# Own tokens' queries ahead of the dense ones, 432 dense columns, and GpSimd on nine pairs' low parts

## The chip, the cores and the metric

One Trainium2 chip, of which the kernel uses one core. The metric is the device time of one launch in microseconds. Engines are named as in the profile: PE is TensorE (PEld its weight loads), DVE is VectorE, ACT is ScalarE, POOL is GpSimd, SP is the engine that issues most transfers.

## The reference

One layer of a streaming encoder over 640 tokens: 512 of a prompt and 128 of eight short samples. A recurrent group and an attention group are merged into h; then each token picks experts. Only that second half changes here:

```python
xn = rmsnorm(h, ln2_g)                                     # 640 x 1024
q = (xn @ w_query).reshape(T, 8, 2, 128)                   # w_query 1024 x 2048
s1 = einsum('thd,kd->thk', q[:, :, 0], sub_keys1)          # 128 keys for each half
s2 = einsum('thd,kd->thk', q[:, :, 1], sub_keys2)
# top 16 of each half, top 16 of the 256 sums: 16 of 16384 experts for each of 8 heads
gates = softmax(top_s)
act = gelu(einsum('thkd,td->thk', u[idx], xn))
y = h + einsum('thk,thkd->td', gates * act, v[idx])
```

## The kernel before

The tokens are five tiles of 128: prompt tiles 0 to 3, and tile 4 with the samples. They take one of two ways through the experts.

*Dense tokens.* The first SD = 448 tokens of the prompt multiply all 16384 experts. The experts come in 64 pairs of 128-column blocks. In the **U stage** (loop over c in 0..63) a pair's weights, 128x2048, are loaded (`u_load`), rounded by ScalarE into the high part wh (`high`, L95) and subtracted into the low part wl (`low`, L100); both together are a `put`. `u_block` (L960) multiplies each block in 24 matmuls of 448 columns: wh with the high and the low part of the tokens, wl with the high part. ScalarE applies gelu into `act`, which goes to memory (Ad). In the **V stage** the same is done for V: activations and gate weights come back (at, gt), are multiplied (`weigh`) and split (`weigh_split`: ph, pl), and `expert_out` (L1359) accumulates 48 matmuls of 448 columns a pair into eight banks. Tiles wh, wl and raw have two buffers each.

*Gate weights.* `select(t)` finds a tile's sixteen experts for each head; `matrix(t)` spreads the weights into a 128x128 map for each token in blocks of eight (`hot` on VectorE, `place` on TensorE, `store` on ScalarE). These pieces have costs in us, and a plan distributes them over the steps of the U loop.

*Own tokens.* The last 64 prompt tokens (HD) and the 128 samples gather their experts' rows instead: for each of NR = 128 + 64 slots GpSimd gathers a row for each partition (`fetch`, L1174), VectorE multiplies it with the token's row (L1181, dots), and later adds the weighted V rows (L1186). A prompt token takes two partitions with 64 rows each, a sample one with 128. `own_work` issues about three gathers a step into a ring of six buffers and consumes those of the step before.

*The query stage* stands ahead of U. Eight slabs of w_query (128x2048, two halves u of 128 columns each) multiply all 640 tokens: `proj_T` (L113) issues 48 matmuls of 320 columns for each u. Behind them `query_keys(u - 2)` scores the queries of two blocks ago against the keys (L914, five tiles), ScalarE copies the scores (L916), VectorE searches them (five instructions a tile). Then, for even u, `next_slab(G)` rounds the next slab on ScalarE and makes its low part on GpSimd; at last `query_out` copies the queries out of PSUM. Each engine runs its instructions in the order in which the code issues them. GpSimd makes the low parts of the query slabs and of the pairs up to 3, VectorE the others.

Of the kernel before, what the change touches and what calls it, by code (L numbers as in the profile page):

```python
# [7 lines left out]
F32 = mybir.dt.float32  # L8
# [8 lines left out]
P = 128  # L17
# [18 lines left out]
SD = S - HD  # L36
# [12 lines left out]
def hybrid_layer(ctx: ExitStack, tc: tile.TileContext, i, o):  # L49
# [144 lines left out]
    for k in range(KD):  # L194
# [19 lines left out]
        + [i["w_out"][n] for n in range(4)] + [i["w_query"][n] for n in range(PH)]  # L214
# [603 lines left out]
    X3 = dram.tile([HD, D], F32, name="X3")  # L818
# [21 lines left out]
    for t in range(NT):  # L840
        merge_attn(0, t)
    next_slab(V)
    for t in range(ND):
        merge_attn(1, t)
        nc.sync.dma_start(Hd[t], h_rows[:, t])
        if t:
            scaled(t - 1)
        mean_square(t)
    merge_attn(1, 4)
    xh, xl = parts_tile()  # L850
    two = [wide(), wide()]
# [25 lines left out]
    sp_ = ctx.enter_context(tc.tile_pool(name="own", bufs=1))  # L877

# [5 lines left out]
    for r in (0, HD):  # L884
        nc.sync.dma_start(xrow[r:r + HD, 1], X3)
    NR = PH * TK + HD
# [3 lines left out]
    ring2 = sp_.tile([P, RING - ND + 1, D], F32, name="ring2")  # L890
    ap_ = ctx.enter_context(tc.tile_pool(name="ap", bufs=2))
# [8 lines left out]
    tq, close_tq = open_pool("tq")  # L900
    qt = {}

    def query_out(u, ps):
        q = qt[u] = tq.tile([P, T], F32, name="q", tag="q", bufs=2)
        A.activation(q.rearrange("p (a b) -> p a b", a=2), ps[:, :, :H2], AF.Copy)

    def query_keys(u):
        c, n = u // 2, u % 2
        s = tq.tile([P, NT, NK], F32, name="s", tag="s", bufs=2)
        q = qt.pop(u)  # L910
        for t0, t1 in ((0, 4), (4, 5)):
            sc = bank()[:, :(t1 - t0) * P]
            for t in range(t0, t1):
                PE.matmul(sc[:, (t - t0) * P:(t - t0 + 1) * P], q[:, t * P:(t + 1) * P], sk[n],  # L914
                          start=True, stop=True)
# [549 lines left out]
```

## Time and profile before

| | |
|---|---|
| timed runs | 1716.91, 1719.96, 1726.47 us (median 1719.96) |
| profiled execution | 1711.95 us, of it span 1710.2 us |
| TensorE busy | 1679.2 us, 98% |
| VectorE, GpSimd, ScalarE busy | 1417.1, 690.2, 679.6 us |
| moved by DMA | 492.67 MB, mean 288 GB/s |
| mean granted TensorE clock | 0.994 of 2.4 GHz |

A line of the profile names an instruction by its line in the kernel, its engine, its operation and its tiles, output first. A matmul's length includes the time through the array, so that neighbours overlap: how fast they follow each other is read from their starts. Lengths on VectorE overlap a little as well. "waits" and "<-" name what an instruction waited for.

### The profile page before, as it was taken

The page shows a single profiled execution, that of the slowest core. Times are in us where ns is not written, and L with a number is a line of the kernel's source. Part 1 is how long each engine was busy: PE and PEld are TensorE (multiplying, and loading weights), DVE is VectorE, ACT ScalarE, POOL GpSimd, SP SyncE. Part 2 cuts the span into 40 slices and gives each one's busy share as a digit, 9 for nine tenths or more (in the row PEclk, how much of TensorE's full clock was granted, in tenths as well). Part 3 has the DMA queues.
Part 4 walks back from the last instruction along what each step waited for, and adds up shares of the span by engine and source line. Part 5 has one row for each costly group of instructions (what it writes and reads, how often), then busy time and mean ns, then how long its engine had stood idle before and what let it go on. Part 6 is the DMA issues. An engine that isn't in the chain of part 4 may idle for free.

```text
span 1710.2 us, 24851 instructions
## 1 busy us (share of the span) xinstructions
PE 1679.2 (98%) x9654; PEld 1546.7 (90%) x9654; DVE 1417.1 (83%) x2348; ACT 679.6 (40%) x790; POOL 690.2 (40%) x485
## 2 busy tenths in 40 slices
PE   8999999999999999999999999899999999999998
PEld 8887889999989898999899999899998999999998
DVE  7766465999789999899988885788887888888886
ACT  5457332233444544554455553322232232232322
POOL 4122003233134344444444433455454555455551
PEclk9999899999999999999999999999999999999999
DMA  5313233223689898999999999999999999999995
GB/s 169 104 48 113 76 105 90 75 70 126 249 277 322 308 377 291 370 389 348 314 379 344 372 352 403 397 380 368 384 374 335 405 376 385 375 377 376 369 350 201
DMA packets 180983, 492.67 MB, mean 288 GB/s; under 512 B 16817, under 2 KB 75057, under 8 KB 170225
## 3 DMA queue, kind: packets, MB, share of 16 engines
q1 hardware_dynamic: 124848, 288.68, 46.7%
q0 software_dynamic: 55296, 201.35, 31.4%
q8 instruction: 75, 1.23, 0.3%
q10 hardware_dynamic: 720, 1.05, 0.2%
q14 instruction: 44, 0.35, 0.1%
HBM read 426.11 MB, written 65.48 MB: 287 GB/s over the span
## 4 chain that ended last, share of the span: by engine, by line
PE 75%; DVE 14%; DMA 5%; ACT 3%; issue 2%; POOL 0%; DVEq 0%; ACTq 0%; SPq 0%
PE po L1359 35%; PE pa L960 21%; PE pa L113 7%; PE pb L1134 3%; DVE wl L100 2%; DMA gt<-Gd 2%; PE pb L638 2%; PE pa L638 2%; DVE ring L1181 2%; DVE h_rows L1181 2%; DMA raw<-in_u 2%; PE pb L914 1%; PE pa L857 1%; ACT wh L95 1%; DMA Gd<-stage 1%
## 5 line engine op out<-in xcount | busy, mean ns | idle before, releaser
L1359 PE MATMUL po<-ph,wh 128*128 128x448 f32 x1024 | 374.7, 366 | 3.5 <-ACT act L1280 1.9
L1359 PE MATMUL po<-pl,wh 128*128 128x448 f32 x1024 | 374.9, 366 | 3.2 <-DVE pl L1273 3.2
L100 DVE TENSOR_TENSOR wl<-raw,wh 128x2048 fp32r<-128x2048 f32 x135 | 308.8, 2288 | 83.5 <-ACT wh L95 82.8
L960 PE MATMUL pa<-xh,wh 128*128 128x448 f32 x1024 | 377.5, 369 | 0.0
L1359 PE MATMUL po<-ph,wl 128*128 128x448 f32 x1024 | 374.5, 366 | 0.0
L960 PE MATMUL pa<-xh,wl 128*128 128x448 f32 x1024 | 374.2, 365 | 0.2 <-DVE wl L100 0.2
L960 PE MATMUL pa<-xl,wh 128*128 128x448 f32 x1024 | 374.1, 365 | 0.0
L95 ACT ACTIVATE wh<-raw 128x2048 fp32r<-128x2048 f32 x146 | 279.5, 1914 | 226.9 <-PE po L1359 173.8
L1174 POOL DMA_INDIRECT h_rows<-in_u_rows,rowi x96 | 138.5, 1443 | 219.9 <-DVE h_rows L1181 164.1
L1174 POOL DMA_INDIRECT ring<-in_u_rows,rowi x96 | 136.8, 1425 | 194.3 <-DVE ring L1181 173.4
L1174 POOL DMA_INDIRECT h_rows<-in_v,rowi x96 | 155.9, 1624 | 143.4 <-DVE h_rows L1186 121.3
L1359 PEld LDWEIGHTS po<-ph,wh 128*128 128x128 f32 x1024 | 192.7, 188 | 19.5 <-ACT act L1280 2.2
L1359 PEld LDWEIGHTS po<-pl,wh 128*128 128x128 f32 x1024 | 192.7, 188 | 19.0 <-DVE pl L1273 3.8
L960 PEld LDWEIGHTS pa<-xh,wl 128*128 128x128 f32 x1024 | 192.3, 188 | 16.1 <-DVE wl L100 0.6
L1359 PEld LDWEIGHTS po<-ph,wl 128*128 128x128 f32 x1024 | 192.7, 188 | 15.3
L960 PEld LDWEIGHTS pa<-xh,wh 128*128 128x128 f32 x1024 | 192.4, 188 | 15.2 <-ACT act L1280 0.3
L960 PEld LDWEIGHTS pa<-xl,wh 128*128 128x128 f32 x1024 | 192.5, 188 | 15.1
L1174 POOL DMA_INDIRECT ring<-in_v,rowi x96 | 149.8, 1560 | 133.2 <-DVE h_rows L1186 109.2
L1280 ACT ACTIVATE act<-pa 128x448 f32<-128x448 f32 x128 | 71.5, 559 | 232.4 <-PE pa L960 225.1
L1271 ACT ACTIVATE ph<-at 128x896 fp32r<-128x896 f32 x64 | 61.0, 953 | 254.0 <-DVE at L1266 254.0
L1142 ACT ACTIVATE stage<-pb 128x512 f32<-128x512 f32 x112 | 109.8, 1129 | 89.9 <-PE pb L1134 89.9
L1273 DVE TENSOR_TENSOR pl<-at,ph 128x896 fp32r<-128x896 f32 x64 | 69.9, 1093 | 72.7 <-ACT ph L1271 72.7
(280 smaller groups left out, 2498.7 us busy)
## 6 DMA issues: line engine op xcount, KB each, us to landing
raw<-in_u SPq DMA_DIRECT2D x64, 1024.0 KB
raw<-in_v SPq DMA_DIRECT2D x64, 1024.0 KB
Ad<-act SPq DMA_DIRECT2D x64, 448.0 KB
Gd<-stage SPq DMA_DIRECT2D x28, 1024.0 KB
gt<-Gd SPq DMA_DIRECT2D x64, 448.0 KB
at<-Ad SPq DMA_DIRECT2D x64, 448.0 KB
raw<-in_w_query SPq DMA_DIRECT2D x8, 1024.0 KB
raw<-in_w_out SPq DMA_DIRECT2D x4, 1024.0 KB
```

Of the source, the lines that this page charges most:

```text
L95: A.activation(wh, raw, AF.Copy)
L100: eng.tensor_sub(wl, raw, wh.bitcast(F32))
L113: PE.matmul(ps[:, hf, :H2], a[:, k, cs], b[:, k, hf * H2:(hf + 1) * H2], start=(k == 0 and n == 0), stop=(k == KD - 1 and n == 2))
L638: PE.matmul(ps, a[:, k0 + k, ts_], b[:, k, :], start=(k == 0 and n == 0), stop=(k == CT - 1 and n == 2))
L960: PE.matmul(u_ps[c, n][:, :SD], a[:, k, n * P:(n + 1) * P], b[:, k, :SD], start=(k == 0 and m == 0), stop=(k == KD - 1 and m == 2))
L1142: A.activation(d["stage"][:, :, t0:t0 + 4].rearrange("p j t -> p t j"), d[n, f], AF.Copy, scale=1.0 / GSC)
L1174: G.indirect_dma_start(out=rows[n], out_offset=None, in_=table, in_offset=bass.IndirectOffsetOnAxis(ap=rowi[:, c:c + 1], axis=0))
L1181: V.scalar_tensor_tensor(row, row, 1.0, xrow[:, n // NS_], op0=ALU.mult, op1=ALU.mult, accum_out=dots[:, n:n + 1])
L1271: A.activation(ph, a2, AF.Copy)
L1273: V.tensor_sub(pl, a2, ph.bitcast(F32))
L1280: A.activation(act[c][:, n], u_ps[c, n][:, :SD], AF.Gelu_apprx_tanh)
L1359: PE.matmul(po[k][:, :SD], a[:, j, k * P:(k + 1) * P], b[:, j, :], start=(c == 0 and j == 0 and n == 0), stop=(c == NS - 1 and j == 1 and ...
```

## The change

Own tokens are now the 128 samples, the last 64 prompt tokens as before, and sixteen more prompt tokens ahead of these (NC). These sixteen gather by head: partition h*16 + t holds head h of token t, in sixteen more slots. Dense tokens are the first 432.

The queries are made in two passes over the eight slabs, which are loaded and split twice: first the 256 columns of tiles 3 and 4 (OWN), then the 384 of tiles 0 to 2 (DENSE). The rows of tiles 3 and 4 are normalised and transposed first. The samples' selection runs in the second pass, and the first ten gathers are issued there. Scores of the dense tiles are held in the buffers of `stage`, and searched partly in the second pass, partly as seven more pieces of the plan. GpSimd makes the low parts of the expert pairs up to 9. The multiplies of the sixteen tokens need the rows by head (`rows_by_head`, eight transfers in the U loop); their sums over heads are made by way of memory (Yc) in the V loop.

```diff
-SD = S - HD
+NC = 16
+C0 = P - HD - NC
+SD = S - HD - NC
...
-        + [i["w_out"][n] for n in range(4)] + [i["w_query"][n] for n in range(PH)]
+        + [i["w_out"][n] for n in range(4)] + [i["w_query"][n] for _ in range(2) for n in range(PH)]
...
+    turns = (ND - 1, ND) + tuple(range(ND - 1))
...
+    OWN, DENSE = slice((ND - 1) * P, T), slice(0, (ND - 1) * P)
+    def queries(ps, w, n, cols):
+        wh, wl = w
         for k in range(KD):
             for m, (a, b) in enumerate(((wh, xh), (wh, xl), (wl, xh))):
+                PE.matmul(ps[:, :cols.stop - cols.start], a[:, k, n * P:(n + 1) * P], b[:, k, cols],
                           start=(k == 0 and m == 0), stop=(k == KD - 1 and m == 2))
...
+    turn_rows(ND - 1)
+    turn_rows(ND)
+    scaled(turns[-1])
     for n in range(2):
+        queries(two[n], kc(slabs[A0 + 2]), n, OWN)
+        turn_rows(n)
+    turn_rows(2)
...
-    for u in range(2, 2 * PH):
-        c, n = u // 2, u % 2
-        ps = wide()
-        proj_T(ps, kc(slabs[Q0 + c]), xh, xl, n)
-        query_keys(u - 2)
-        if n == 0:
-            if c + 1 < PH:
-                next_slab(G)
...
-        query_out(u, ps)
...
+    for u in range(2, 2 * PH):
+        ps = wide()[:, 0]
+        queries(ps, kc(slabs[Q0 + u // 2]), u % 2, OWN)
+        own_keys(u - 2)
+        if u % 2 == 0:
+            next_slab(G)
+        query_out(u, ps, OWN)
+    todo, acts, sought, used = list(own_first), [], 0, 0.0
+    for u in range(2 * PH):
+        c, n = u // 2, u % 2
...
+        queries(ps, kc(slabs[Q0 + PH + c]), n, DENSE)
+        if u < 2:
+            own_keys(2 * PH - 2 + u)
+        else:
+            scores(u - 2 + 2 * PH, 3, later(u - 2))
+        for f in acts:
+            f()
+        if n == 0:
+            if c + 1 < PH:
+                next_slab(G)
...
+        query_out(u + 2 * PH, ps, DENSE)
+        used = max(used, 0.0) - 4.2
+        while used < 0:
+            if todo:
+                p = todo.pop(0)
+                p[2]()
...
+            elif sought < u - 2:
+                search(sought, tiles, held_s[sought])
...
+        if not todo:
+            own_step(n_pre, n_pre + 1)
+            n_pre += 1
...
+            if n == NB_ - 1:
+                rows_by_head()
...
+            if c == NR - 1:
+                nc.sync.dma_start(Yc.rearrange("h (t q) d -> (h t) (q d)", t=NC), y)
+                parts = p2.tile([P, PH, P], F32, name="parts", tag="y2")
+                nc.sync.dma_start(parts, Yc.rearrange("h r d -> r h d"))
+                rest = p2.tile([P, 2, P], F32, name="rest")
...
+                V.tensor_reduce(rest[:, 1], parts.rearrange("p h d -> p d h"), axis=AX.X, op=ALU.add)
+                V.tensor_add(rest[:, 0], rest[:, 0], rest[:, 1])
...
-            put(*((U, c + 1) if c + 1 < NS else (Pv, 0)), G if c <= 2 else V)
+            put(*((U, c + 1) if c + 1 < NS else (Pv, 0)), G if c <= 8 else V)
```

ScalarE's order in the query stage, before, from the rounding of one slab to that of the next (s are scores, q queries, wh a slab's high part):

```order
L95 ACTIVATE wh<-raw 128x2048
L905 ACTIVATE q<-pa 128x640
L916 ACTIVATE s<-pb 128x512
L916 ACTIVATE s<-pb 128x128
L905 ACTIVATE q<-pa 128x640
L916 ACTIVATE s<-pb 128x512
L916 ACTIVATE s<-pb 128x128
L95 ACTIVATE wh<-raw 128x2048
```

The same of the changed kernel in the pass over the own columns (the tile act now holds queries, out of pa, and scores, out of pb):

```order
L97 ACTIVATE wh<-raw 128x2048
L932 ACTIVATE act<-pa 128x256
L940 ACTIVATE act<-pb 128x256
L932 ACTIVATE act<-pa 128x256
L940 ACTIVATE act<-pb 128x256
L97 ACTIVATE wh<-raw 128x2048
```

The sequence is the same, with 256 columns where there were 640; the rounding stands behind a copy of scores in both.

GpSimd's order before, from its last low parts to the gathers of the first steps:

```order
L100 TENSOR_TENSOR wl<-raw,wh 128x2048 x2
L1174 DMA h_rows<-in_u_rows,rowi 128x1024 x3
L1174 DMA ring_2608<-in_u_rows,rowi 128x1024 x3
L1174 DMA h_rows<-in_u_rows,rowi 128x1024 x3
L1174 DMA ring_2608<-in_u_rows,rowi 128x1024 x3
```

And of the changed kernel, from the end of the second query pass into the U loop:

```order
L102 TENSOR_TENSOR wl<-raw,wh 128x2048
L1185 DMA h_rows<-in_u_rows,rowi 128x1024
L1185 DMA ring_2561<-in_u_rows,rowi 128x1024
L102 TENSOR_TENSOR wl<-raw,wh 128x2048
L1185 DMA ring_2561<-in_u_rows,rowi 128x1024 x2
L1185 DMA h_rows<-in_u_rows,rowi 128x1024
L102 TENSOR_TENSOR wl<-raw,wh 128x2048
L1185 DMA h_rows<-in_u_rows,rowi 128x1024 x2
```

Low parts and gathers now alternate, where all low parts stood ahead of all gathers.

VectorE's order in the V loop of the changed kernel, at the sixteen tokens' last sum (yc is their sum, parts what comes back from memory):

```order
L102 TENSOR_TENSOR wl<-raw,wh 128x2048
L1351 TENSOR_TENSOR at<-at,gt 128x864
L1358 TENSOR_TENSOR pl<-at,ph 128x864
L1202 SCALAR_TENSOR_TENSOR yc<-ring_2561,slots,yc 128x1024
L1215 TENSOR_REDUCE rest<-parts 128x128
L1216 TENSOR_TENSOR rest<-rest 128x128
L1202 SCALAR_TENSOR_TENSOR h_rows<-h_rows,slots 128x1024 x2
L102 TENSOR_TENSOR wl<-raw,wh 128x2048
L1351 TENSOR_TENSOR at<-at,gt 128x864
```

The reduction and the addition behind it are new; the low part of the next pair and its weighing stand behind them.

## Rows read from the trace of the kernel before

**Rows 1.** Stage by stage; times in us, TensorE clock, DMA share.
```profile
core 0: us, PE busy (x) PEld busy (x) DVE busy (x) ACT busy (x) POOL busy (x), PEclk, DMA share, GB/s
268.00:383.00 115.00, 115.00 (x822) 115.00 (x821) 96.86 (x522) 31.96 (x50) 32.39 (x7) 1.00 0.20 66
383.00:1071.00 688.00, 681.50 (x3993) 626.73 (x3991) 608.79 (x1129) 328.03 (x344) 278.02 (x192) 1.00 0.91 327
1071.00:1703.00 632.00, 626.85 (x3091) 580.01 (x3091) 535.00 (x416) 185.24 (x136) 319.22 (x201) 1.00 0.96 366
620.00:1000.00 380.00, 377.97 (x2353) 348.53 (x2352) 349.19 (x503) 194.99 (x204) 164.59 (x113) 1.00 0.98 351
```

**Rows 2.** First and last dense matmul of each stage, durations in ns.
```profile
L960 PE MATMUL pa<-xh,wh x1024: 362/365/472, 383.0 to 1068.6; 128*128 128x448 f32 x171
...
L1359 PE MATMUL po<-ph,wh x1024: 362/365/575, 1071.3 to 1702.2; 128*128 128x448 f32 x171
```

**Rows 3.** Timeline of one slab's period in the query stage; start, length in us.
```profile
267.94 0.46 PE L113 MATMUL pa<-xh,wh 128*128 128x320 f32 x2
...
274.98 1.27 PE L914 MATMUL pb<-sk,q 128*128 128x128 f32 x10
276.07 0.77 ACT L916 ACTIVATE s<-pb 128x512 f32<-128x512 f32 x2 [7.23 <-PE pb L914]
276.72 1.92 ACT L95 ACTIVATE wh<-raw 128x2048 fp32r<-128x2048 f32 x1
278.71 4.63 POOL L100 TENSOR_TENSOR wl<-raw,wh 128x2048 fp32r<-128x2048 f32 x1 [11.53 <-ACT wh L95]
...
284.17 0.54 PE L113 MATMUL pa<-xh,wh 128*128 128x320 f32 x2
```

**Rows 4.** GpSimd's low parts, shortest, median and longest in ns.
```profile
L100 POOL TENSOR_TENSOR wl<-raw,wh x11: 4612/4626/4649, 262.5 to 406.3; 128x2048 fp32r<-128x2048 f32 x11
```

**Rows 5.** Timeline, starts of matmuls of 256, 512, 320 and 448 columns.
```profile
100.08 0.28 PE L186 MATMUL pb<-wl,xh 128*128 128x256 f32 x1
...
102.60 0.28 PE L186 MATMUL pb<-wl,xh 128*128 128x256 f32 x1
...
227.81 1.07 PE L638 MATMUL pb<-wh,xl 128*128 128x512 f32 x4
...
230.53 1.07 PE L638 MATMUL pa<-wh,xl 128*128 128x512 f32 x4
...
274.69 0.46 PE L113 MATMUL pa<-xh,wl 128*128 128x320 f32 x2
...
1199.82 0.36 PE L1359 MATMUL po<-pl,wh 128*128 128x448 f32 x1
...
1204.48 0.36 PE L1359 MATMUL po<-ph,wh 128*128 128x448 f32 x1
```

**Rows 6.** Chain of waits, TensorE's placing of two blocks in the U stage.
```profile
689.44 1.85 PE pb L1134 x32
```

**Rows 7.** Timeline, ScalarE spreading a selection.
```profile
430.78 3.70 ACT L1048 ACTIVATE ix<-it 128x2048 f16<-128x2048 f16 x2
```

**Rows 8.** Stretches around a fall of TensorE's clock, columns as Rows 1.
```profile
160.00:165.00 5.00, 2.96 (x23) 1.66 (x21) 4.13 (x8) 3.24 (x5) 5.00 (x8) 1.00 0.98 359
165.00:170.00 5.00, 4.37 (x9) 2.01 (x8) 5.00 (x5) 4.97 (x14) 2.15 (x2) 0.60 0.58 211
170.00:175.00 5.00, 5.00 (x74) 4.25 (x74) 4.72 (x9) 0.12 (x1) 0.00 (x0) 0.50 0.01 3
```

**Rows 9.** Groups by line, VectorE, 620 to 1000 us.
```profile
L100 DVE TENSOR_TENSOR wl<-raw,wh 128x2048 fp32r<-128x2048 f32 x35 | 80.1, 2290 | 26.6 <-ACT wh L95 26.1 <-issue 0.4
...
L1181 DVE SCALAR_TENSOR_TENSOR h_rows<-h_rows,xrow 128x1024 f32<-128x1024 f32 x56 | 66.4, 1222 | 0.0
```

**Rows 10.** Timeline, VectorE in V behind a transfer.
```profile
1312.39 1.22 DVE L1190 TENSOR_TENSOR h_rows<-h_rows,y 64x1024 f32<-64x1024 f32 x1 [3.00 <-DMA y<-h_rows]
```

**Rows 11.** Instructions on one tile, 400 to 412 us, lengths in ns.
```profile
L1004 DVE TENSOR_TENSOR cand<-val x4: 209/312/4659, 406.4 to 411.5; 128x128 f32<-128x128 f32 x2, 128x192 f32<-128x192 f32 x1, 128x64 f32<-128x64 f32 x1
```

More of the change, by code (lines that the diff above doesn't have):

```diff
@@ L1149, in matrix, with later, rest_of_plan @@
             piece(2.4, lambda n=n: hot(n), pe=lambda n=n: place(n), act=lambda n=n: store(n))
-    for t in (ND, ND - 1):
-        select(t)
-    n_own = len(pieces)
-    select(0)
-    matrix(ND - 1)
-    select(1)
-    matrix(0)
-    select(2)
-    matrix(1)
-    matrix(2)
+    select(ND)
+    own_first = pieces[:]
+    del pieces[:]
+    held, held_s = [], {}
+    def later(u):
+        if u == 2 * PH - 1:
+            held_s[u] = qs[u + 2 * PH][:, 3 * P:6 * P]
+        else:
+            if u % 5 == 0:
+                held.append(tb.tile([P, NK, TG], F32, name="stage", tag="stage", bufs=3)
+                            .rearrange("p a b -> p (a b)"))
+            held_s[u] = held[u // 5][:, u % 5 * 3 * P:(u % 5 + 1) * 3 * P]
+        return held_s[u]
+    def rest_of_plan():
+        select(ND - 1)
+        select(0)
+        matrix(ND - 1)
+        select(1)
+        matrix(0)
+        select(2)
+        matrix(1)
+        matrix(2)
     NO = 2 * NR
-    NS_ = PH * TK
     rows = {}
@@ L1198, in hybrid_layer, with own_step @@
     NS = NK // 2
[L1201 to L1229 removed]
+    n_pre = 0
+    def own_step(n0, n1):
         for n in sorted(rows):
@@ L1235, in own_work, with own_keys @@
             fetch(n)
+    def own_work(c):
+        own_step(*[n_pre + min(NO - n_pre, (NO - n_pre) * x // (2 * NS - 2)) for x in (c, c + 1)])
+    Q0 = A0 + 2
+    own_tiles, tiles = (ND - 1, ND), tuple(range(ND - 1))
+    def own_keys(u):
+        s = qs[u][:, 2 * P:4 * P]
+        scores(u, 2, s)
+        search(u, own_tiles, s)
+    next_slab(G)
+    for u in range(2):
+        query_out(u, two[u], OWN)
+    for u in range(2, 2 * PH):
[5 more added lines that the diff above has]
+        query_out(u, ps, OWN)
@@ new lines, in hybrid_layer @@
+    put(U, 1, G)
+    scores(4 * PH - 2, 3, later(2 * PH - 2))
+    u_block(0, 0)
+    scores(4 * PH - 1, 3, later(2 * PH - 1))
+    for u in (2 * PH - 1, *range(sought, 2 * PH - 1)):
+        piece(5.0, lambda u=u: search(u, tiles, held_s[u]))
+    rest_of_plan()
+    plan = [[] for _ in range(NS + 4)]
+    total = sum(p[0] for p in pieces)
+    used, c = 0.0, 0
+    for p in pieces:
+        while used >= total * (c + 1) / (NS - 6):
+            c += 1
+        plan[c].append(p)
+        used += p[0]
+        if p[5]:
+            c += 1
```

175 lines of the change are left out of this document (79 added, 96 removed).

## The prediction

> **What bounds the kernel now.** I read the table of stages first, then the first and last dense matmuls, then the query stage instruction by instruction, then what VectorE and GpSimd do beside the dense stages.
>
> [rows 1] is to be read as three stages. In the query stage (268 to 383 us) TensorE is busy for all of 115.0 us; in the U stage (383 to 1071) for 681.5 of 688; in the V stage (1071 to 1703) for 626.85 of 632. [rows 2] gives the same borders from the matmuls themselves. So TensorE bounds all three, and each matmul made shorter is a gain as long as nothing else becomes late. What could become late is to be seen in [rows 1] and [rows 3]. In the U stage VectorE has 349.19 us of work in a stretch of 380, the DMA engines a share of 0.91 to 0.98. In the query stage the slab chain is nearly as long as TensorE's own work: TensorE starts a slab at 267.94, its scores at 274.98; ScalarE copies the scores at 276.07, only then rounds the next slab (276.72, 1.92 us), GpSimd starts on the low part at 278.71 and ends at 283.34, and TensorE takes up that slab at 284.17. That chain has 0.83 us to spare in a slab period of 16.23 us. TensorE does not wait there today only because a slab gives it sixteen microseconds of matmuls.
>
> **The change, part by part.**
>
> *Columns.* 3072 matmuls of U and 3072 of V go from 448 to 432 columns. The starts in [rows 5] give the pitch: 256 columns 120.0 ns (21 steps from 100.08 to 102.60), 512 columns 226.7 ns (12 steps), 320 columns 146.7 ns (46 steps from 267.94 of [rows 3] to 274.69), 448 columns 202.6 ns (23 steps). The first three are exactly 32 columns more than the width at 2.4 GHz; 448 is 2.6 ns above that. I keep the 2.6 ns and take 16/2.4 = 6.67 ns off each: 6144 x 6.67 ns = -41.0 us. Ends: -37 by the slope from 448 to 512 (6.0 ns), -57 if 432 lands on the rule (193.3 ns, so 9.3 ns).
>
> *Placing.* Two of the 56 blocks of eight tokens go. Two blocks cost 1.85 us of TensorE [rows 6]: -1.9 us.
>
> *Query stage.* This is the large term. The queries are now done in two passes over the same eight slabs, 256 own columns first, then 384 dense ones, and each slab is loaded, rounded and split twice. The order on ScalarE has not changed in kind: copy of the scores, rounding of the next slab, copy of the queries. So the next slab's rounding still waits until TensorE has done one query block and the scores behind it, but TensorE has now only the second block with which to cover rounding and low part. The period from one slab's low part to the next's, own pass: 22 remaining matmuls x 0.120 = 2.64, scores of two tiles 0.51 (ten instructions take 1.27 [rows 3]), hand-over 0.07, copy of 256 columns 0.30 (640 take 0.65), rounding and hand-over 1.99, low part 4.63 ([rows 4]: 4,612 to 4,649 ns in all eleven), 0.05: 10.2 us, against 6.8 us of TensorE's work. Dense pass: 22 x 0.1733 = 3.81, scores 0.76, 0.07, 0.40, 1.99, 4.63, 0.05: 11.7 us against 9.8. ScalarE also spreads the selection of the sample tile ahead of one rounding, 3.7 us [rows 7]. The first slab that the loop makes is ready at about 268 in both kernels, for its rounding stands behind the copies of the last transposes in both. So U starts at 268 + 7 x 10.2 + 8 x 11.7 + 3.7 = 437, not 383.0: +54 us. Nothing hides this: TensorE's next instruction needs that slab. Ends: +11 if no slab were late (7 x 6.8 + 8 x 9.8 = 126 us instead of 115), +54 otherwise. I take +54, since each link of the chain has its row.
>
> *TensorE's clock.* The own pass leaves gaps of 3.4 us in every 10.2. The nearest rows are [rows 8]: after five microseconds in which TensorE was busy for 2.96 the granted clock went from 1.00 to 0.60 in the next five and 0.50 (1.2 GHz) in those after. At 1.2 GHz an own period would be 22 x 0.12 + 0.51 = 3.15 us longer. Ends 0 and 7 x 3.15 = +22; I take +3, one period, for the gap ahead of the first slab that the loop makes, which is twice as long.
>
> *U stage.* Nine pairs' low parts (2.29 us each on VectorE, three of them on GpSimd already) leave VectorE, 16 more gathers and seven leftover searches come in. Behind the ninth pair VectorE's work per pair is what it was: 349.19 us over 35 pairs ([rows 1], [rows 9]), 9.98 us, plus 0.2 because by the planner's own costs 256.6 units fill 58 steps where 203.4 filled 48. TensorE's pair falls from 380/35 = 10.86 to 10.54. The margin goes from 0.88 to 0.36 us a pair. Today TensorE idles 6.5 us in this stage; with the margin more than halved I take that to grow by as much again and a little, +8 us. Ends: -6.5 (the relief of nine pairs removes all waits) and +20.
>
> *Transfers that VectorE now waits for.* Between dots 192 and 193 eight transfers rewrite the own rows; the next multiply waits for them. In V the 16 gathered tokens' sums go to memory and back, two transfers one behind the other, before a VectorE reduction; queued behind that reduction are the next pair's low part and weighing, and TensorE waits for those. The nearest row is the one transfer of that kind that there is: VectorE sat 3.00 us [rows 10]. I take +3 for the first (0 to 10) and +8 for the second, two such waits of double size less the slack of a pair (3 to 20).
>
> *Nothing.* The earlier start of the gathers, the 8 MB of second slab loads and the GpSimd gathers between low parts are hidden: the loads have a 10 us period at 66 GB/s [rows 1], and in the dense pass GpSimd has 4.63 + 2 gathers in 11.7 us.
>
> *Sum.* -41.0 - 1.9 + 54 + 3 + 8 + 3 + 8 = +33.1 us. On the profiled execution's 1711.95 us (span 1710.2) that is 1745 us. The timed runs of before lie at 1716.9 to 1726.5, their median 8.0 above the profiled execution, so I expect 1753 us in timed runs.
>
> **Rivals.**
>
> *The slabs are not late* (faster). TensorE's work is all that counts, as today, where the stage has no idle microsecond [rows 1]. Then +54 and +3 become +11: -41 - 1.9 + 11 + 19 = -13, 1699, timed 1707. It decides if the slab period is under 6.8 and 9.8 us; for that the rounding would have to run before the scores' copy, and the order says otherwise. Against it stands the 0.83 us that the chain has to spare now.
>
> *It comes back in the dense stages* (no change). The columns cost 193.3 ns (-57) and the relief of VectorE takes away the waits of U (-6.5) and most of the transfers' (+5): -57 - 1.9 + 57 - 6.5 + 5 = -3, timed 1717. The 2.6 ns above the rule speak for it, VectorE's share for the rest of U against it.
>
> *GpSimd holds VectorE* (slower still). The one VectorE instruction with two inputs from SBUF that met a low part on GpSimd lasted 4,659 ns where its fellows last about 0.3 us [rows 11]; it ended with the low part. If the row multiplies of the pairs 1 to 8 are held like this, each pair has 3.8 us of multiplies (3.2 of 1.19 us, [rows 9]), 4.1 of search (three tiles; in the query stage 70 tiles took 96.86 us [rows 1]) and up to 4.63 of holding, 12.5 us against TensorE's 48 x 0.196 = 9.4: 8 x 3.1 = +25, timed 1778. It decides where VectorE has no search to put beside the low part; the order puts the multiplies right behind it, so I expect most of the holding to fall where a search would have run anyway.
> The Trainium skill's GPSIMD Engine Reference, section Specifications, says that GpSimd's way into SBUF is shared with VectorE and that instructions with two SBUF inputs contend for it. By that rule every row multiply beside a low part would wait, and the time would be the 1778 us of this rival; the trace agrees with its 4,659 ns for one instruction, and shows no row multiply in that place.
>
> *The DMA engines become the bound* (slower still). V moves 366 GB/s at a share of 0.96 [rows 1]. If that is the most they give, 16 more gathers of 0.52 MB less 2 MB of narrower tiles are 6 MB, 16 us, and V takes 648 us instead of 632 - 20: +36, timed 1789. That TensorE idles only 5 us in V today, at whatever rate the transfers ask for, speaks against it.
>
> **Chances.** Forecast 0.64, slabs not late 0.08, comes back 0.12, GpSimd holds 0.10, DMA 0.06. The forecast alone runs from 1725 (columns at -57, the small terms at their low ends less half) to 1780 (clock and U at their high ends). The range for all is 1718 to 1788. About 0.5%, 8.6 us, is what a measurement of this kernel can tell from no change. Faster 0.08; same 0.11, from the third case and the forecast's edge; slower 0.81.
>
> **What would show it.** TensorE's busy time between the first own query and the first 432-column matmul should be about 70 to 85% with gaps ended by GpSimd's low part, 3.4 us each in the own pass and 1.9 in the dense; the first 432-column matmul should start near 437; 432 columns should have a pitch of 195.9 ns; U should take about 674 us and V about 620; GpSimd's 25 low parts should last 4.6 us each. I am wrong if TensorE stays busy through both passes, if the pitch is not between 193 and 197, or if the pairs 1 to 8 of U take 12 us and more.

## The result and the profile after

The changed kernel took 1787.11 us (median of four runs, 1777.9 to 1791.96) against 1721.49 us before (median of four, 1716.91 to 1726.47): a ratio of 1.037 with a 95% interval of 1.032 to 1.043. Slower was forecast and slower it is, but 1753 us was too little: the measured change, 65.6 us, is twice the forecast one. Its profiled execution took 1789.18 us, 77.2 us above that of before.

The table of stages of the changed kernel, for the stretches that answer to [rows 1], columns as there:

```profile
268.00:454.70 186.70, 144.84 (x873) 140.89 (x873) 118.49 (x549) 53.19 (x78) 78.11 (x24) 0.88 0.30 108
454.70:1151.00 696.30, 668.04 (x3956) 632.27 (x3955) 622.36 (x1157) 316.91 (x335) 340.12 (x218) 0.99 0.95 339
1151.00:1780.00 629.00, 610.99 (x3085) 584.12 (x3086) 532.90 (x404) 182.80 (x134) 309.15 (x201) 0.98 0.96 365
```

and the first and last dense matmul of each stage, answering to [rows 2]:

```profile
L958 PE MATMUL pa<-xh,wh x1024: 351/360/710, 454.7 to 1149.8; 128*128 128x432 f32 x171
...
L1444 PE MATMUL po<-ph,wh x1024: 351/358/729, 1151.2 to 1780.1; 128*128 128x432 f32 x171
```

The query stage was without an idle microsecond before. Now TensorE is busy for 144.8 of its 186.7 us, at a mean granted clock of 0.88. Counting 48 matmuls to a pair in the timeline splits the whole difference:

| from, to | before | after | change |
|---|---|---|---|
| start to first U matmul | 383.0 | 454.7 | +71.7 |
| U, 64 pairs | 686.4 | 695.9 | +9.5 |
| between U and V | 1.9 | 0.6 | -1.3 |
| V, 64 pairs | 631.7 | 629.6 | -2.1 |
| behind V | 7.3 | 6.6 | -0.7 |

An undisturbed pair takes 9.40 us in U and 9.36 in V, where it took 9.73 in both: 64 x (0.33 + 0.37) = 44.8 us that the columns do bring. U and V together are 7.4 us longer all the same, so 52 us are lost in them again. Most of it, some 40 us, lies in pairs that stand far apart: of U those that start at 587, 601, 614 and 1085 us (14.1, 13.1, 13.6 and 18.5 us), of V those at 1334, 1349, 1390 and 1407 (14.2, 13.2, 17.3 and 12.9).

**The slab chain**, answering to [rows 3]. One undisturbed period of the pass over the own columns, timeline, start and length in us:

```profile
306.07 0.39 PE L866 MATMUL pa<-xh,wl 128*128 128x256 f32 x1 [3.32 <-POOL wl L102]
308.81 0.61 PE L939 MATMUL pb<-sk,act 128*128 128x128 f32 x4
309.45 0.39 ACT L940 ACTIVATE act<-pb 128x256 f32<-128x256 f32 x1 [6.24 <-PE pb L939]
309.74 1.91 ACT L97 ACTIVATE wh<-raw 128x2048 fp32r<-128x2048 f32 x1
311.72 4.53 POOL L102 TENSOR_TENSOR wl<-raw,wh 128x2048 fp32r<-128x2048 f32 x1 [5.70 <-ACT wh L97]
316.30 0.39 PE L866 MATMUL pa<-xh,wl 128*128 128x256 f32 x1 [3.33 <-POOL wl L102]
```

The links follow one another as in [rows 3], but the period is now the chain's own length, 10.23 us, and TensorE waits 3.33 us in it. What was not expected is what happens to periods like this one elsewhere. Three stretches of ten microseconds of the changed kernel, columns as above:

```profile
280.00:290.00 10.00, 8.24 (x48) 8.24 (x49) 3.58 (x20) 2.35 (x3) 1.80 (x2) 0.66 0.29 105
310.00:320.00 10.00, 6.67 (x57) 6.47 (x56) 5.95 (x32) 2.88 (x6) 4.53 (x1) 1.00 0.31 97
430.00:440.00 10.00, 10.00 (x52) 10.00 (x52) 3.86 (x17) 2.67 (x3) 3.25 (x3) 0.83 0.56 210
```

At 280 us and again at 430 the mean clock lies between its two levels (0.5 would be 1.2 GHz all through). The matmuls ahead of the scores then take longer, and the scores, the copy, the rounding and the low part all come later: the slab chain starts on TensorE, so a slow TensorE lengthens it. Three of the seven own periods took 11.6 to 12.7 us and six of the dense ones 13.3 to 14.0, where the chain alone makes 10.2 and 11.8 (the latter from e2 below).

**The exchange by way of memory in V**, timeline of the changed kernel:

```profile
1390.29 0.32 SPq L1210 DMA_DIRECT2D Yc<-yc  x1
1392.93 0.37 SPq L1212 DMA_DIRECT2D parts<-Yc  x1
1398.00 1.96 DVE L1215 TENSOR_REDUCE rest<-parts 128x128 f32<-128x1024 f32 x1 [7.74 <-DMA parts<-Yc]
1400.00 0.29 DVE L1216 TENSOR_TENSOR rest<-rest 128x128 f32<-128x128 f32 x1
1400.32 0.34 SPq L1217 DMA_DIRECT2D out_y<-rest  x1
1400.75 0.39 SPq L92 DMA_DIRECT2D raw<-in_v  x1
1401.19 0.66 SPq L1340 DMA_DIRECT2D gt<-Gd  x1
1404.93 1.05 DVE L1351 TENSOR_TENSOR at<-at,gt 128x864 f32<-128x864 f32 x1
1406.15 0.92 ACT L1356 ACTIVATE ph<-at 128x864 fp32r<-128x864 f32 x1 [14.36 <-DVE at L1351]
1407.12 0.73 PE L1444 MATMUL po<-ph,wh 128*128 128x432 f32 x1 [7.74 <-ACT ph L1356]
```

VectorE waits 7.74 us for the transfer, and TensorE waits as long, 7.74 us, nine microseconds later, for what stood behind the reduction on VectorE: low part and weighing. SyncE is held too, from 1393.9 to 1400.3, by the store of the sum, and the next loads stand behind it; no run separates this hold from VectorE's wait. The pair after the wait takes 12.9 us instead of 9.4, at a clock of 0.74. The other exchange, that of the prompt's last tokens ([rows 10], 3.00 us there), does the same at 1348.58: TensorE waits 4.12 us, and the next pair takes 13.2.

**Small transfers in U.** The sixteen tokens' slots and rows are spread over the heads by transfers of their own:

```profile
594.65 5.24 SPq L1088 DMA_DIRECT2D slots<-ts  x8
...
600.57 5.22 SPq L1088 DMA_DIRECT2D rowi<-ti  x8
605.88 0.53 SPq L92 DMA_DIRECT2D raw<-in_u  x1
...
611.89 1.91 ACT L97 ACTIVATE wh<-raw 128x2048 fp32r<-128x2048 f32 x1 [9.98 <-DMA raw<-in_u]
...
614.27 0.47 PE L958 MATMUL pa<-xh,wh 128*128 128x432 f32 x1 [3.53 <-ACT act L1365]
```

SyncE issues one in 0.65 us; with two more of their kind they keep it for twelve microseconds, and a slab of U is asked for only behind them. ScalarE has nothing to round for 9.98 us. And at the rows by head:

```profile
1081.44 4.39 SPq L893 DMA_DIRECT2D xrow<-X  x8
...
1092.34 1.23 DVE L1192 SCALAR_TENSOR_TENSOR h_rows<-h_rows,xrow 128x1024 f32<-128x1024 f32 x1 [10.93 <-DMA Gd<-stage]
...
1096.03 1.25 PE L1131 MATMUL pb<-ow,oh 128*128 128x128 f16 x10 [6.27 <-DVE ow L1123]
```

The multiply reads xrow and a gathered row, never Gd: the transfer named in the bracket is only the one that ended nearest. It waits for the eight copies ahead of it, 10.93 us, and the placing that TensorE waits for stands behind it on VectorE.

**GpSimd**, one of the pairs 3 to 10 of U:

```profile
485.20 1.97 POOL L1185 DMA_INDIRECT ring<-in_u_rows,rowi  x1 [0.30 <-issue]
487.47 0.93 POOL L1185 DMA_INDIRECT h_rows<-in_u_rows,rowi  x1 [0.30 <-DVE s L925]
488.41 4.63 POOL L102 TENSOR_TENSOR wl<-raw,wh 128x2048 fp32r<-128x2048 f32 x1
491.00 3.14 DVE L1192 SCALAR_TENSOR_TENSOR ring<-ring,xrow 128x1024 f32<-128x1024 f32 x1
493.20 1.77 POOL L1185 DMA_INDIRECT h_rows<-in_u_rows,rowi  x1 [0.16 <-issue]
495.27 1.97 POOL L1185 DMA_INDIRECT h_rows<-in_u_rows,rowi  x1 [0.30 <-issue]
497.54 0.93 POOL L1185 DMA_INDIRECT ring<-in_u_rows,rowi  x1 [0.30 <-DVE s L925]
498.49 4.62 POOL L102 TENSOR_TENSOR wl<-raw,wh 128x2048 fp32r<-128x2048 f32 x1
```

From one low part to the next GpSimd has 10.08 us without a pause: 4.63 and three gathers, two of which take 1.8 to 2.0 us beside a multiply on VectorE and one 0.93 beside a search. TensorE needs 9.40, so that the low part is late from pair 6 on, by 0.7 us a pair.

### The profile page after: what moved, and what is told of

The parts are those of the page before. It is cut to its first block, busy times and chain, and to the rows that moved or that the text cites. A ratio compares the mean times of both kernels' runs of the same rounds, so it can differ in the third digit from the quotient of the medians.

```text
span 1787.4 us, 25007 instructions
## 1 busy us (share of the span) xinstructions
PE 1672.1 (94%) x9622; PEld 1576.3 (88%) x9622; DVE 1450.1 (81%) x2391; ACT 687.0 (38%) x808; POOL 788.5 (44%) x531
## 4 chain that ended last, share of the span: by engine, by line
DVE 40%; PE 28%; DMA 12%; issue 9%; ACT 5%; POOL 5%; SPq 1%; ACTq 0%; DVEq 0%; POOLq 0%
DVE wl L102 11%; DVE h_rows L1202 7%; PE pa L958 7%; PE po L1444 6%; PE pa L866 5%; DVE ring L1192 4%; DMA raw<-in_u 4%; DVE h_rows L1192 4%; POOL wl L102 4%; DMA raw<-in_v 3%; DVE at L1351 3%; ACT ph L1356 2%; PE pa L115 2%; ACT wh L97 1%; PE pb L640 1%
## 5 line engine op out<-in xcount | busy, mean ns | idle before, releaser
L1444 PE MATMUL po<-ph,wh 128*128 128x432 f32 x1024 | 369.5, 361 | 12.5 <-ACT ph L1356 11.9
L958 PE MATMUL pa<-xh,wl 128*128 128x432 f32 x1024 | 370.6, 362 | 8.9 <-DVE wl L102 5.8
L958 PE MATMUL pa<-xh,wh 128*128 128x432 f32 x1024 | 372.8, 364 | 3.5 <-ACT act L1365 3.5
L1444 PE MATMUL po<-pl,wh 128*128 128x432 f32 x1024 | 370.4, 362 | 5.9 <-DVE pl L1358 5.9
L958 PE MATMUL pa<-xl,wh 128*128 128x432 f32 x1024 | 369.4, 361 | 0.0
L1444 PE MATMUL po<-ph,wl 128*128 128x432 f32 x1024 | 368.9, 360 | 0.0
L1444 PEld LDWEIGHTS po<-pl,wh 128*128 128x128 f32 x1024 | 194.6, 190 | 17.1 <-DVE pl L1358 9.8
L958 PEld LDWEIGHTS pa<-xh,wh 128*128 128x128 f32 x1024 | 195.1, 191 | 11.3 <-ACT act L1365 3.9
L958 PEld LDWEIGHTS pa<-xl,wh 128*128 128x128 f32 x1024 | 195.1, 190 | 7.3
L1356 ACT ACTIVATE ph<-at 128x864 fp32r<-128x864 f32 x64 | 59.3, 926 | 325.7 <-DVE at L1351 317.2
L1365 ACT ACTIVATE act<-pa 128x432 f32<-128x432 f32 x128 | 69.5, 544 | 240.6 <-PE pa L958 238.0
L102 POOL TENSOR_TENSOR wl<-raw,wh 128x2048 fp32r<-128x2048 f32 x25 | 114.7, 4589 | 107.0 <-ACT wh L97 106.7
L1192 DVE SCALAR_TENSOR_TENSOR h_rows<-h_rows,xrow 128x1024 f32<-128x1024 f32 x105 | 129.9, 1268 | 26.6 <-DMA h_rows<-in_u_rows,rowi 15.6
## 6 DMA issues: line engine op xcount, KB each, us to landing
at<-Ad SPq DMA_DIRECT2D x64, 432.0 KB, 10.3
```

The lines of the kernel that those rows point to most:

```text
L102: eng.tensor_sub(wl, raw, wh.bitcast(F32))
L958: PE.matmul(u_ps[c, n][:, :SD], a[:, k, n * P:(n + 1) * P], b[:, k, :SD], start=(k == 0 and m == 0), stop=(k == KD - 1 and m == 2))
L1192: V.scalar_tensor_tensor(row, row, 1.0, xrow[:, n // NS_], op0=ALU.mult, op1=ALU.mult, accum_out=dots[:, n:n + 1])
L1356: A.activation(ph, a2, AF.Copy)
L1365: A.activation(act[c][:, n], u_ps[c, n][:, :SD], AF.Gelu_apprx_tanh)
L1444: PE.matmul(po[k][:, :SD], a[:, j, k * P:(k + 1) * P], b[:, j, :], start=(c == 0 and j == 0 and n == 0), stop=(c == NS - 1 and j == 1 and ...
```

## The experiments

All ratios are to the kernel before, as it was timed beside each experiment; its medians lie between 1715 and 1721 us, so times of different experiments are compared through the ratios or by stage. Several kernels repeat the query stage of the changed one to the letter, and its first U matmul then lay at 454.7, 455.0, 456.9 and 463.4 us: what that stage does from run to run is nearly as much as a mended wait of U or V brings, so the edits in U and V are read from their own stage, counted by pairs as in the table above, and not from the total.

**e1, the rounding ahead of the scores.** In both passes:

```diff
-        own_keys(u - 2)
         if u % 2 == 0:
             next_slab(G)
+        own_keys(u - 2)
         query_out(u, ps, OWN)
```

> The changed kernel with one thing reordered in both query passes: the rounding of the next slab (ScalarE) and its low part (GpSimd) are issued ahead of the scores of the block before, not behind their copy. Theory (the slab chain is late because the rounding stands behind the scores' copy): rounding starts when the slab before last is done, 0.3 + 1.97 + 4.6 = 6.9 us for a slab against 6.8 us of TensorE in the own pass and 9.8 in the dense one; the gaps go, the clock stays at 1.00, the first 432-column matmul starts near 269.8 + 7 x 6.95 + 8 x 9.8 + 3 = 400 us instead of 454.7, and the time falls by about 55 us to 1733. Rival (GpSimd's own rate, or the loads, or a clock that stays low for another reason set the period): the own period stays at 10 us and the dense one at 13, first 432-column matmul above 440, time 1775 or more.

Measured: 1748.21 us, ratio 1.016 [1.010, 1.021]. The first U matmul starts at 407.8 us, 46.9 earlier, at a clock of 0.95:

```profile
268.00:407.80 139.80, 129.60 (x873) 128.81 (x873) 117.37 (x490) 53.22 (x78) 85.78 (x26) 0.95 0.44 151
407.80:1115.50 707.70, 672.65 (x3956) 636.97 (x3954) 638.23 (x1218) 315.68 (x335) 331.39 (x217) 0.97 0.93 333
```

The time lies between the theory's 1733 and the rival's 1775, the start of U near the theory's 400. So the place of the rounding on ScalarE was the cause, and low part and loads were not. But U is longer by 11.4 us (707.3, by pairs): VectorE comes into it with more to do (638.23 us busy in U, 622.36 in the changed kernel), the searches that the shorter stage left it no time for. The clearest wait shows it. TensorE stands 5.68 us at 478.56 for a low part of GpSimd, which stood behind a gather that had waited for a VectorE multiply. A quarter of the gain in the query stage is given back there.

**e2, needless matmuls in the gaps.** 24 of 256 columns, or 8 of 384, in front of each slab's first block:

```diff
-    def queries(ps, w, n, cols):
+    def queries(ps, w, n, cols, fill=0):
...
+        for _ in range(fill):
+            PE.matmul(ps[:, :cols.stop - cols.start], wh[:, 0, n * P:(n + 1) * P], xh[:, 0, cols],
+                      start=True, stop=True)
         for k in range(KD):
```

> The changed kernel with needless matmuls put in front of each slab's first query block (24 of 256 columns in the own pass, 8 of 384 in the dense one), on operands that are ready, into the PSUM tile that the real block then overwrites: they fill 2.9 of the 3.3 us gap and 1.4 of the 1.9 us gap, and take nothing from the path if the slab's low part is what TensorE waits for. Theory (part of the query stage's excess is TensorE's clock, which falls behind the gaps): the granted clock stays at 1.00 through both passes, the own periods that took 11.6 to 12.7 us fall to 10.2 and the dense ones from 13.4 to 11.7, the first 432-column matmul comes at about 438 us instead of 454.7, and the time falls by some 16 us to 1771. Rival (the excess is the chain's, longer links than I took): periods stay at 13.4 in the dense pass with the clock at 1.00, and the time stays at 1787 or rises.

Measured: 1779.37 us, ratio 1.035 [1.030, 1.041]. The clock is 1.00 in stretches where it was 0.66 and 0.83 above:

```profile
280.00:290.00 10.00, 9.47 (x80) 9.27 (x80) 5.80 (x31) 2.81 (x6) 4.61 (x1) 1.00 0.30 105
...
430.00:440.00 10.00, 8.68 (x53) 8.36 (x52) 8.31 (x38) 3.06 (x5) 7.35 (x3) 1.00 0.32 109
```

By the starts of GpSimd's low parts the seven own periods now take 72.0 us in all (77.2 in the changed kernel) and the eight dense ones 102.5 (109.4). So 12.1 us of the stage were the clock, and doing more work made it shorter. The total is down by less, 7.3 us at the first U matmul, because ahead of the first slab the fillers did not stand in a gap: that low part starts at 270.08, not 265.24. The first U matmul, at 447.4 us, and the time lie between theory and rival.

**e3, the exchanges in V cut in two.** Addition, reduction and store move to the next pair:

```diff
-                V.tensor_add(y[HD:], y[HD:], y2[HD:])
-                nc.sync.dma_start(o["y"][ND - 1][HD:], y[HD:])
+                def added():
+                    V.tensor_add(y[HD:], y[HD:], y2[HD:])
+                    nc.sync.dma_start(o["y"][ND - 1][HD:], y[HD:])
+                after_step.append([added])
...
     def own_step(n0, n1):
+        for f in after_step.pop(0) if after_step else ():
+            f()
```

> The changed kernel with the two exchanges by way of memory in the V loop cut in two: the transfers to and from memory are issued where they were, but VectorE's addition and reduction and the store behind them are issued one pair later. Theory (SyncE holds a store that waits for VectorE, which waits for the transfer; the next loads stand behind it, so that TensorE waits, and its clock falls): the pairs that took 14.2 + 13.2 and 17.3 + 12.9 us take 9.4 to 9.8 each, V shrinks from 629 to about 609 us, the time falls by 17 to 20 us to about 1769. Rival (the DMA engines, at a share of 0.96, bound V and any relief comes back elsewhere): V stays above 622 us, time within 7 us of 1787.

Measured: 1781.5 us, ratio 1.035 [1.029, 1.041]; V by pairs 615.6 us, 14.0 less. Of these 3.1 lie in V's first pair, which the edit doesn't touch and which took 11 to 17 us in the other kernels. The four pairs took 10.0, 10.4, 10.1 and 12.1 us, and the one behind them 12.0, for the wait is shorter but not gone:

```profile
1400.19 1.99 DVE L1220 TENSOR_REDUCE rest<-parts 128x128 f32<-128x1024 f32 x1 [1.89 <-DMA parts<-Yc]
...
1410.67 0.46 PE L1454 MATMUL po<-ph,wh 128*128 128x432 f32 x1 [2.61 <-ACT ph L1366]
```

The theory holds in its stage, to some 11 of the expected 20 us. The total shows only 5.6, the rival's number: in the profiled execution the query stage, which the edit doesn't touch, was 8.7 us longer.

**e4, the small transfers one to a pair**, and the rows by head into the samples' rows:

```diff
-                        nc.sync.dma_start(dst[h * NC:(h + 1) * NC, NB_:], src[C0:HD, h * TK:(h + 1) * TK])
+                        spread_out.append((dst[h * NC:(h + 1) * NC, NB_:], src[C0:HD, h * TK:(h + 1) * TK]))
...
-            nc.sync.dma_start(xrow[h * NC:(h + 1) * NC, 1], X3[:NC])
+            spread_out.append((xrow[h * NC:(h + 1) * NC, 0], X3[:NC]))
...
-            if n == NB_ - 1:
+            if n == NS_ - 1:
                 rows_by_head()
...
+        due = [spread_out.pop(0) for _ in range(min(len(spread_out), 1 if c > 20 else 0))]
         own_work(c)
+        for dst, src in due:
+            nc.sync.dma_start(dst, src)
```

> The changed kernel with the small transfers of the sixteen tokens taken apart: the sixteen transfers that spread their slots and rows over the heads, issued in one piece at 594 us, and the eight that copy their token rows, issued at 1081 us into the rows that VectorE is just done with, are issued one in each pair from pair 21 on, the latter into the samples' rows as soon as these are done. Theory (SyncE issues each in 0.65 us, 12 us in a row, and the loads of the U slabs stand behind them; VectorE waits 10.9 us for the rewritten rows): the pair that starts at 601 and the one at 614 lose the wait and its clock (13.1 and 13.6 us to about 10), the one at 1085 goes from 18.5 to 11.3 us, U shrinks from 696 to 682 us, time about 1774. Rival (VectorE is late there anyway and the loads find the DMA engines full): U shrinks by 7 us or less, time above 1780.

Measured: 1781.71 us, ratio 1.035 [1.029, 1.042]; U by pairs 685.4 us, 10.5 less. The pairs named took 9.40, 9.40 and 10.37 us, 16 less in all; 5.5 of that came back in others (pair 19, and 49 to 53, where the DMA engines are at their busiest), which lies between the two theories. Another 4.3 came back between U and V, where TensorE waits 4.9 us instead of 0.6, so that the first V matmul is only 6 us nearer to the first of U; the time, above 1780, is the rival's.

**e5, GpSimd's low parts up to pair 3 as before.**

```diff
-            put(*((U, c + 1) if c + 1 < NS else (Pv, 0)), G if c <= 8 else V)
+            put(*((U, c + 1) if c + 1 < NS else (Pv, 0)), G if c <= 2 else V)
```

> The changed kernel with GpSimd making the low parts of the expert pairs up to 3 alone, as before; VectorE makes those of pairs 4 to 9 again. Theory (GpSimd is the bound from pair 6 on: 4.62 us of low part and three gathers stretched by VectorE's work make 10.08 us a pair against 9.40 of TensorE): pairs 6 to 10 fall to 9.40 us (-4), but VectorE takes up six low parts, 13.7 us, where it is 93% busy, and the selections of the prompt's tiles come later: pairs 11 to 20 lose 5 to 10 us more, U is 0 to 6 us longer, time 1787 to 1793. Rival (the held multiplies, 2.0 to 4.4 us where their fellows take 1.2, cost VectorE as much as the low parts would): U is 3 us shorter or more, time 1784 or less.

Measured: 1790.44 us, ratio 1.045 [1.041, 1.050]; U by pairs 694.7 us against 695.9. Handing six low parts to GpSimd neither helped nor harmed U. Two of pairs 6 to 10 fell to 9.5 us or less, and pair 13 took 16.3 instead of 14.1, in the direction of the first theory; the rival, with U 3 us shorter, did not come.

**e6, e7, e8, the edits of e1, e3 and e4 together**, with GpSimd's low parts up to pairs 9, 3 and 6.

> The changed kernel with three edits together: next slab's rounding ahead of the scores, the V exchanges cut in two, the small transfers spread over the pairs. Theory (they act in three stages and add): -39 - 14 - 10 by the stages measured apart, so a time near 1724, about that of the kernel before (0.2 to 0.8% above it). Rival (VectorE or GpSimd, behind by what they didn't do in the shorter query stage, gives the gain back in U): U above 707 us, time 1735 or more.

> The same three edits, and GpSimd's low parts up to pair 3 alone, as before. Theory (with a short query stage GpSimd's low parts come late in pairs 2 to 9, since they stand behind gathers that wait for VectorE, and hold VectorE's multiplies to 3 us): without them the first fourteen pairs lose 10 us less, time near 1714. Rival (VectorE is the bound there and has 13.7 us more to do): 1730 or more.

> The same three edits, and GpSimd's low parts up to pair 6. Theory (VectorE bound in the first fourteen pairs): a time between those of the same kernel with limits 2 and 8 for GpSimd. Rival (the two engines share the work best in the middle): 3 us or more below both.

Measured: 1731.44, 1728.87 and 1734.96 us, ratios 1.010 [1.006, 1.013], 1.008 [1.005, 1.010] and 1.010 [1.006, 1.014]. The three edits take 56 of the 66 us back by the times and 48 by the ratios, either way less than the 63 of their stages. Between the three limits there is nothing that these runs can tell apart: e6 lies between its two theories, and neither number of e7 and e8 came. First U matmuls lie at 411.4, 410.0 and 406.6 us, 24 to 28 later than before, and U takes 690.5 to 694.7.

**e11, the spreading of the selection behind the copy of the queries**, on top of e6:

```diff
+        query_out(u + 2 * PH, ps, DENSE)
         for f in acts:
             f()
         acts = []
-        query_out(u + 2 * PH, ps, DENSE)
```

> The changed kernel with the three edits of before (rounding ahead of the scores, exchanges cut in two, small transfers spread), and the spreading of the samples' selection on ScalarE (3.7 us) issued behind the copy of the queries, not ahead of it. Theory (TensorE waits 5.4 us for that copy, once): the gap goes, with its share of low clock, the first 432-column matmul starts 5 to 8 us earlier, near 404 us, time near 1725. Rival (VectorE is behind in the query stage and U gives it back): U longer by as much, time 1729 or more.

Measured: 1727.11 us, ratio 1.004 [1.001, 1.007], first U matmul at 402.8 us, 8.7 earlier than e6, U 689.9. As the theory has it.

**e9, one query pass, the rest of the change kept.** The kernel before, with 432 columns, the sixteen tokens, their transfers and their exchange as the changed kernel has them.

> One part of the change undone: the queries are made in one pass of 640 columns as before, with GpSimd's low parts up to pair 3 and the searches and the samples' selection where they were; the 432 dense columns, the sixteen more gathering tokens, their eight-fold transfers and the exchange by way of memory stay as in the changed kernel. Theory (the two passes cost 55 to 70 us, the columns bring 45, the sixteen tokens' waits take some 30 of these): the first 432-column matmul starts at 383 us again, U takes 680 to 690 us and V 625 to 630, time 1705 to 1720, within 0.5% of before. Rival (the own rows' work, which now starts later and must be done in fewer pairs, holds U, and the earlier start by the two passes was needed): U above 700 us, time above 1728.

Measured: 1739.23 us, ratio 1.010 [1.005, 1.015]; first U matmul 386.8, U 680.7 as expected, but V 656.2 by pairs where 625 to 630 was expected. The time is 48 us below that of the changed kernel (47 by the ratios), and this is a difference of larger numbers: the first U matmul lies 67.9 us earlier and U is 15.2 shorter, but V is 26.6 longer and the step from U to V 7.4. The time is the rival's, but its place is not, since U is short. V went wrong in a way that neither theory had: two pairs of 16.4 and 20.1 us at the exchanges, and every second of the others at 10.3 to 10.4.

**e10, the same with the edits of e3 and e4.**

> The kernel with one query pass and 432 columns, and the sixteen tokens' transfers mended: the small ones spread one to a pair, the token rows by head written early into the samples' rows, the exchanges by way of memory cut in two. Theory (nothing but the columns is then left of the change on the path): U 675 to 682 us, V 612 to 618, time 1688 to 1698, 1.0 to 1.6% below before. Rival (VectorE, with 16 more multiplies in U and the margin per pair down by a half, keeps U where it was): U 686 us or more, time 1705 or more.

Measured: 1716.96 us, ratio 0.999 [0.996, 1.001]; U 676.3 us, as expected, V 642.5 and every second pair still 10.4. One of them, timeline of V:

```profile
1497.63 2.29 DVE L102 TENSOR_TENSOR wl<-raw,wh 128x2048 fp32r<-128x2048 f32 x1
...
1499.83 1.05 DVE L1306 TENSOR_TENSOR at<-at,gt 128x864 f32<-128x864 f32 x1
...
1501.05 0.93 ACT L1311 ACTIVATE ph<-at 128x864 fp32r<-128x864 f32 x1 [6.21 <-DVE at L1306]
1502.01 1.06 DVE L1313 TENSOR_TENSOR pl<-at,ph 128x864 fp32r<-128x864 f32 x1 [1.13 <-ACT ph L1311]
1502.99 3.92 DVE L1206 SCALAR_TENSOR_TENSOR h_rows<-h_rows,slots 128x1024 f32<-128x1024 f32 x3
...
1506.95 1.28 DVE L1206 SCALAR_TENSOR_TENSOR h_rows<-ring,slots,h_rows 128x1024 f32<-128x1024 f32 x1
1508.15 2.28 DVE L102 TENSOR_TENSOR wl<-raw,wh 128x2048 fp32r<-128x2048 f32 x1
```

GpSimd gathers 208 rows in V here, 3.4 a pair, so that about every second pair adds four. VectorE then goes round in 10.52 us, 1.13 of it waiting for ScalarE to round the weights. So it was neither U nor the DMA engines. The changed kernel issues ten gathers ahead of U, has (416 - 10)/126 = 3.2 rows a pair, and only five pairs of V at 9.8 to 10.1 us. With the exchanges cut in two its V takes 615.6 us (e3) and V here 642.5; most of these 27 us are what its early start is worth.

**e12, weighing ahead of the low part**, on top of e10:

```diff
-            put(Pv, c + 1, V)
+            Pv[c + 1][1] = high(Pv[c + 1][0])
             weigh(c + 1)
-            weigh_split(c + 1)
+            a2 = W[c + 1]
...
+            A.activation(ph, a2, AF.Copy)
+            Pv[c + 1][2] = low(Pv[c + 1][0], Pv[c + 1][1], V)
...
+            V.tensor_sub(pl, a2, ph.bitcast(F32))
```

> The kernel with one query pass, 432 columns and the sixteen tokens' transfers mended, with one thing reordered in the V loop: VectorE weighs the next pair ahead of making that pair's low part, so that ScalarE's rounding of the weights runs beside the low part. Theory (V is held in every second pair, 10.38 us instead of 9.40, because VectorE has four row additions there and waits 1.13 us for ScalarE between weighing and the weights' low part: 4 x 1.28 + 2.29 + 1.05 + 1.13 + 1.06 = 10.6; without the wait 9.5): the pairs with four additions fall to 9.4 to 9.6 us, V from 642.5 to about 616 us, time about 1690, 1.3 to 1.7% below the kernel before. Rival (the DMA engines, at a share of 0.97, or the weights' loads set the pair): V stays above 635 us, time 1710 or more.

Measured: 1687.27 us (six runs, 1684.77 to 1689.65), ratio 0.981 [0.978, 0.984]. The low part now lies over ScalarE's rounding:

```profile
1482.23 1.05 DVE L1306 TENSOR_TENSOR at<-at,gt 128x864 f32<-128x864 f32 x1
1483.30 2.29 DVE L102 TENSOR_TENSOR wl<-raw,wh 128x2048 fp32r<-128x2048 f32 x1
...
1483.46 0.93 ACT L1393 ACTIVATE ph<-at 128x864 fp32r<-128x864 f32 x1 [0.19 <-DVE at L1306]
1485.51 1.05 DVE L1396 TENSOR_TENSOR pl<-at,ph 128x864 fp32r<-128x864 f32 x1
```

```profile
383.00:1064.00 681.00, 663.50 (x3962) 629.91 (x3960) 617.68 (x1154) 322.08 (x338) 302.45 (x207) 0.99 0.93 337
1064.00:1680.00 616.00, 606.66 (x3091) 582.68 (x3091) 555.54 (x440) 181.31 (x137) 338.66 (x218) 0.99 0.99 390
```

V takes 612.2 us by pairs. This kernel beats both: 1.9% below the kernel before. In the profiled execution U is 8.0 us shorter than before and V 19.5, while the step between them is 4.2 longer. What the new order in V alone would bring the kernel before was not run; its V lies 9 us above 64 undisturbed pairs, so that it could be a part of the gain, not the whole. It keeps the 432 columns and the sixteen gathering tokens and drops the two query passes and GpSimd's extra low parts. The DMA share of V is 0.99 at 390 GB/s, where [rows 1] have 366 at 0.96, so the rival of the DMA engines falls here as well.

## Why the prediction was right or wrong

*The size.* The profiled execution was forecast at 1745 us and took 1789.18, 44.2 more: 14.7 of these in the query stage (17.7 less the 3 of the clock term), 21.9 in U and 9.6 in V, less 2.0 at the borders. That the timed runs miss by 34 us only, and that 1787 lies inside the range, at its upper edge (1788), is owed to the 8.0 us added for timed runs: the changed kernel's median lies 2.1 us below its profiled execution. None of the three signs of being wrong came, so they did not watch the terms that failed.

*The bound, the order, the sign: right.* TensorE waits in the query stage for GpSimd's low part, with the gaps that were forecast (3.33 us for 3.4 in the own pass, 1.8 to 2.0 for 1.9 in the dense one), TensorE is busy for 78% of it, and e1 shows that ScalarE's order makes them.

*Columns: right.* 195.7 ns in U and 195.1 in V by the mean of the starts, for 195.9; 44.8 us by the pairs for 41.0.

*The query stage, +54: the chain was right, the clock term failed.* First U matmul 454.7 us for 437. The prediction put the clock at +3, "one period", between ends of 0 and +22; by e2 it was 12. The reason given, that only the gap ahead of the first slab is long enough, does not hold: the clock was 0.83 from 430 to 440 us, right behind a gap of 1.96 us, and 0.87 in the other undisturbed periods of the dense pass. Some 5 us more lie in links a little longer than their rows of before, at the pass's beginning and beside the selection (17.1 us for the one period that 15.4 was forecast for).

*U, +8 and +3: the terms that missed most.* 695.9 us for 674. Waits and clock cost some 32 us more than before (9.5 + 64 x 0.33 + 1.9), not 11. The step "transfers that VectorE now waits for" put the eight transfers at +3, with 10 as the most; VectorE sat 10.93 us, and TensorE lost 7.2 us with it. And the sixteen transfers at the selection were not in the sum at all, though the change issues them: twelve microseconds of SyncE, 7.9 us of TensorE (e4). GpSimd's 10.08 us a pair, which was not worked out, stretched pairs 6 to 10 by another 4, though U was only 1.2 us shorter without it (e5). The rest is mostly VectorE, late at the selections between 564 and 680 us; how much of that is the smaller margin the runs don't separate.

*V, +8: the mechanism right, the size wrong.* 629.6 us for 620. The sum took two waits of double size less the slack of a pair. Measured were one wait of TensorE of 7.74 us and one of 4.12, and behind each a pair at a clock of 0.74 that cost 3.5 and 3.8 more: some 20 us over undisturbed pairs, where the kernel before had 3, and of which e3 took 11 away. The prediction's list of what stands behind the reduction was right; that SyncE's store stands ahead of the next loads was not in it, and neither was a clock term for V.

*The rivals.* GpSimd does hold VectorE, but cheaply: of the multiplies beside low parts one a pair is held, 1.4 to 4.4 us where its fellows take 1.22, and ends 1.09 us behind the low part, whenever it began (491.00 above). That is 12 us of VectorE in nine pairs, where the rival had 25 of TensorE in eight. By the Trainium skill's GPSIMD Engine Reference, section Specifications, instructions with two SBUF inputs contend with GpSimd; the trace agrees in the length, and searches beside a low part keep their 0.28 us. Taking six of the low parts back from GpSimd (e5) brought U 1 us. The DMA engines are not the bound, by e12. The slabs were late, so the rival of the faster side fell with the result; that the gain comes back in the dense stages did happen, 52 us against 44.8, but on top of the query stage and not in its place.

## What to carry to other kernels

A wait of TensorE is priced with what its clock does behind it: here some 3.5 us on top of a wait of 4 to 8, and 12 us over a stage that waited a little in every period. A transfer that is exchanged by way of memory is priced on three engines: the one that waits for the data, the queue that holds the store behind it, and the loads behind that store; issuing the second half one step later took 11 of some 20 us back here. And before a stage is split so that each part gives a chain less work to hide behind, look at which instruction starts the chain: moving one rounding ahead of one copy was worth 47 us of that stage.

## What the runs showed of the hardware

Needless matmuls made a stage shorter (e2: 102.5 us instead of 109.4 for eight slabs), by holding the granted clock higher: 1.00 instead of 0.89 from 268 to 342 us, and 0.97 instead of 0.88 from there to the first U matmul. When it falls can't be read from these runs: the same gap of 3.33 us left it at 1.00 from 300 to 345 us and stood beside 0.66 at 280.

A gather that GpSimd issues takes 0.93 us beside a VectorE search and 1.8 to 2.0 beside a VectorE multiply, so that three gathers beside one search and two multiplies keep GpSimd for 5.5 us (488.41 to 498.49 above: 10.08 us less the low part).

A VectorE row multiply that began while GpSimd made a low part ended 1.08 or 1.09 us behind that part, in all eleven cases of the changed kernel.

The V stage moved 390 GB/s in the last kernel, 24 more than before, at a share of 0.99, and TensorE still had 9.40 us pairs.
